# Bias tables read from one reversed line, memory projections ahead of the compressed branch, in a fused two-layer transformer step

## The chip, the cores and the metric

The kernel runs on one core of one Trainium2 chip. The metric is the device time of one execution in microseconds (us), lower is better; the kernel before takes 2472.95 us, the median of three runs.

## The reference, cut to what is computed

Two layers act on one sequence x of 512 positions by 1024 features, with a memory of 256 rows by 1024. The change touches the first layer, between its first feed-forward and its attention:

```python
def hybrid_layer(x, mem, ...):
    x = x + 0.5 * swiglu_ffn(rmsnorm(x, ffn1_norm_g), ffn1_w_in, ffn1_w_out)
    h = rmsnorm(x, mix_norm_g)
    q, kv, nsa_g, conv_in, q_mem, merge_g = jnp.split(h @ w_in, split_points, axis=-1)
    ...
    k_cmp = rmsnorm(compress(kc, cmp_pe_k, cmp_w1_k, cmp_w2_k), k_norm_g)
    v_cmp = compress(vc, cmp_pe_v, cmp_w1_v, cmp_w2_v)
    o_nsa = nsa_attention(q, k_cmp, v_cmp, ..., gates, rel_bias)
    o_conv = short_gated_conv(conv_in, conv_w, conv_b)
    o_mem = memory_attention(q_mem, mem, mem_norm_g, w_mem_kv, mem_q_norm_g, mem_k_norm_g)
    x = x + (g_nsa * o_nsa + g_conv * o_conv + g_mem * o_mem) @ w_out
    return x + 0.5 * swiglu_ffn(rmsnorm(x, ffn2_norm_g), ffn2_w_in, ffn2_w_out)

def memory_attention(q_mem, mem, mem_norm_g, w_mem_kv, q_g, k_g):
    km, vm = jnp.split(rmsnorm(mem, mem_norm_g) @ w_mem_kv, 2, axis=-1)
    km = rmsnorm(km.reshape(b, m, MEM_HEADS, MEM_HEAD_DIM), k_g)      # 4 heads of 256
    qm = rmsnorm(q_mem.reshape(b, s, MEM_HEADS, MEM_HEAD_DIM), q_g)
    sm = jnp.einsum('bshd,bmhd->bhsm', qm, km) * MEM_HEAD_DIM ** -0.5
    return jnp.einsum('bhsm,bmhd->bshd', jax.nn.softmax(sm), vm)
```

The scores of `nsa_attention` get a bias `rel_bias[rel_bucket(t - pos)]`, one value for each head and distance. The second layer has its own mixer and feed-forward (f3, after a cross attention); nothing of it is moved.

## The kernel before, in words

Activations lie transposed: eight tiles `X[k]` of 128 features by 512 positions. Each fp32 operand of a product is split into a high and a low part in a short float type (`split`, `w`), and a product is three matmuls: high by high, high by low, low by high. A weight unit of 128x1024 elements (512 KB) is loaded by SyncE's (SP's) DMA queue into one of three buffers `wr` (`raw`, L305), cast to `wh` by ScalarE (`copy`, L260), and `wl = wr - wh` is computed by GpSimd for two units of three and by VectorE for the third, inside the mixer (`wes`). `chunk` then issues 24 matmuls for one unit: of 512 columns for products with x, of 256 for products with the memory.

A scheduler puts the instructions of each engine in an order from the order of the program, the tile buffers and the priorities given; it may let an instruction come earlier than its place in the code. `tick` takes one closure from a list `todo` and runs it at the place of the call.

The stages that matter, in the order of time:

- `ffn("f1", ...)`: the first feed-forward, in three groups of hidden units. The last group's eight output products end at 362.5 us. `form_x` makes combinations of x for a Strassen-like product, early in a feed-forward.
- `mix1`, compressed branch (`compressed`): `cmp_src` makes four projections of x and multiplies each with the row factors `rb` of the norm; `cmp_blocks` writes VectorE's `zr` tiles from them; `compress` multiplies those with `cw1`. Between them `mem_q` makes the memory queries (`m1_qm`). Meanwhile `mem_prep` scales and splits the memory rows (`mh`, `ml`) and computes their norm, a step at each `tick` of `mem_q`.
- memory projections (`mem_kv`): eight units `m1_km` for the keys, eight `m1_vm` for the values, the sums of squares `ksq` for the keys' norm, and eight small products with `bm` that spread the norm's factors over the keys. At the ticks of the key units the bias tables are made (`tables`): a product of a one-hot array `oh1` with the bias table `rel` gives `drel`, a line of 640 values by head in DRAM; GpSimd's queue then copies the line to 128 rows of `dline` for each head, two heads to a DMA of 640 KB, eight DMAs. A second one-hot `oh2` gives `dcmp` for the compressed branch.
- memory heads (`mem_heads`): for each of four heads two gate units `m1_gm`, the scores (`softmax_mem`: VectorE's minimum, ScalarE's exponential `pm`), the transposes (`turn_mem`) and the product with the values. Query products of the attention follow, to 654.4 us.
- attention (`nsa`): 660 to 1120 us. `nsa_scores` loads for each head a tile `tab` of 128x512 biases, row p shifted by p, from `dline`, one head ahead (two buffers), and VectorE reads it once for each of the eight score tiles of a head (`sp<-s,tab`, L1274), adding it and taking the minimum in one pass.

## Time and profile before

| | |
|---|---|
| median of 3 runs | 2472.95 us (2469.25 to 2478.96) |
| the profiled execution | 2475.88 us, its span 2474.1 us |
| mean granted clock of TensorE | 0.977 of full speed |
| TensorE (PE) busy | 2373.4 us, 96% of the span |
| VectorE (DVE) busy | 1691.0 us, 68% |
| ScalarE (ACT) busy | 1160.3 us, 47% |
| GpSimd (POOL) busy | 435.1 us, 18% |

A row of a busy-time table gives, for a stretch, the busy time of each engine, the granted clock as a share of 2.4 GHz, the share of the DMA engines' time and what they moved. A row of a timeline is one instruction or a run of equal ones; in brackets stands the idle time of its engine before it and the instruction that ended that idle time. The durations of matmuls overlap, so their sum over a stretch is more than its length; how fast TensorE goes is read from how many lie in a stretch.

### The profile page before, as it was taken

Reading aid. Unit: us, or ns where it says so; the run is one execution under the profiler, and the core shown is the slowest. Engines: PE = TensorE matmul, PEld = TensorE weight load, DVE = VectorE, ACT = ScalarE, POOL = GpSimd, SP = SyncE. Lnnn points to the kernel's source line nnn. Section 1 sums busy time; section 2 is a strip of 40 time slices with the busy share of each in tenths; the row PEclk is TensorE's granted clock in tenths of the full one; section 3 lists DMA queues with packets and bytes.
Section 4 is the critical chain, followed back from the end, with each engine's and each line's share of the span. In section 5 each row is a group of like instructions: output and inputs, shape, how many; then the busy total and the mean of one; then the engine's idle time right before and its main releaser. Section 6 shows DMA issues by size and latency. Waiting matters only on the chain.

```text
span 2474.1 us, 35466 instructions
## 1 busy us (share of the span) xinstructions
PE 2373.4 (96%) x13618; PEld 2055.2 (83%) x13618; DVE 1691.0 (68%) x3150; ACT 1160.3 (47%) x2084; POOL 435.1 (18%) x266
## 2 busy tenths in 40 slices
PE   8999998969999999999999999998999998999997
PEld 6999987857777878787899898797788887899997
DVE  7766878544578676877767685467877357867675
ACT  6534453334355444554544353454655345644353
POOL 0000003331222223222000002121211431000000
PEclk9999999789999999999999999899999998999998
DMA  6545543352222222224455543122122332555551
GB/s 190 174 132 154 156 142 103 115 160 70 77 75 69 69 74 73 67 66 150 118 155 152 156 139 119 62 75 71 60 77 71 115 122 77 137 163 145 158 142 55
DMA packets 99486, 277.44 MB, mean 112 GB/s; under 512 B 18017, under 2 KB 26145, under 8 KB 99188
## 3 DMA queue, kind: packets, MB, share of 16 engines
q1 hardware_dynamic: 82660, 239.81, 29.6%
q0 software_dynamic: 16656, 35.36, 7.7%
q8 instruction: 107, 1.75, 0.3%
q14 instruction: 63, 0.52, 0.1%
HBM read 268.68 MB, written 11.64 MB: 113 GB/s over the span
## 4 chain that ended last, share of the span: by engine, by line
PE 64%; DVE 11%; ACT 3%; issue 3%; DMA 1%; POOL 1%; DVEq 0%; ACTq 0%; POOLq 0%
PE g L231 36%; PE s L231 12%; PE t L231 11%; PE o L231 3%; PE t L239 2%; DVE wl L242 2%; ACT wh L260 1%; DVE qk L242 1%; DMA wr<-f_s 0%; POOL wl L242 0%; DVE sp L1274 0%; DVE cv L254 0%; DMA wr<-m_gm 0%; DMA wr<-f_o 0%; DMA wr<-m_vm 0%
## 5 line engine op out<-in xcount | busy, mean ns | idle before, releaser
L231 PE MATMUL g<-xs,wh 128*128 128x512 f32 (+1 forms) x3022 | 875.9, 372 | 10.3 <-ACT wh L260 6.0
L260 ACT CAST wh<-wr 128x1024 fp32r<-128x1024 f32 (+6 forms) x405 | 409.9, 1016 | 612.8 <-PE g L231 217.9
L231 PEld LDWEIGHTS g<-xs,wh 128*128 128x128 f32 x3022 | 541.9, 190 | 100.7 <-ACT wh L260 11.2
L231 PE MATMUL g<-xs,wl 128*128 128x512 f32 (+1 forms) x1511 | 559.5, 370 | 1.9 <-POOL wl L242 1.2
L242 POOL TENSOR_TENSOR wl<-wr,wh 128x1024 fp32r<-128x1024 f32 (+4 forms) x135 | 313.0, 2320 | 918.0 <-ACT wh L260 754.9
L242 DVE TENSOR_TENSOR wl<-wr,wh 128x1024 fp32r<-128x1024 f32 (+5 forms) x270 | 327.1, 1213 | 65.8 <-ACT wh L260 63.4
L231 PEld LDWEIGHTS g<-xs,wl 128*128 128x128 f32 x1511 | 286.0, 189 | 51.1 <-issue 2.4
L231 PE MATMUL s<-xs,wh 128*128 128x256 f32 (+1 forms) x890 | 223.8, 340 | 5.5 <-ACT xs L260 2.0
L231 PE MATMUL t<-xs,wh 128*128 128x512 f32 (+1 forms) x888 | 222.2, 340 | 0.0
L565 POOL DMA_DIRECT2D wr<-f_s x57 | 49.4, 866 | 843.6 <-DMA wr<-f_s 232.1
L231 PEld LDWEIGHTS s<-xs,wh 128*128 128x128 f32 x890 | 153.2, 190 | 27.4 <-ACT wh L260 2.9
L231 PEld LDWEIGHTS t<-xs,wh 128*128 128x128 f32 x888 | 152.7, 189 | 18.6 <-ACT e L260 0.4
L231 PE MATMUL t<-xs,wl 128*128 128x512 f32 (+1 forms) x444 | 150.8, 340 | 2.7 <-DVE wl L242 2.7
L231 PE MATMUL s<-xs,wl 128*128 128x256 f32 (+1 forms) x445 | 150.4, 338 | 0.0
L257 ACT ACTIVATE sp<-sp,nm 128x128 f32<-128x128 f32 x192 | 101.9, 532 | 54.4 <-DVE nm L1274 41.6
L242 DVE TENSOR_TENSOR ptl<-t,pth 128x512 fp32r<-128x512 f32 (+1 forms) x128 | 73.4, 604 | 55.3 <-ACT pth L260 55.0
L260 ACT CAST pth<-t 128x512 fp32r<-128x512 f32 (+1 forms) x128 | 62.0, 520 | 92.4 <-PE t L239 92.0
L231 PEld LDWEIGHTS t<-xs,wl 128*128 128x128 f32 x444 | 83.7, 189 | 12.9 <-DVE wl L242 3.6
L231 PEld LDWEIGHTS s<-xs,wl 128*128 128x128 f32 x445 | 84.4, 190 | 8.9
L231 PE MATMUL g<-th,wl 128*128 128x256 f32 x308 | 86.6, 281 | 1.3 <-DVE wl L242 1.0
L231 PE MATMUL g<-th,wh 128*128 128x256 f32 x308 | 85.9, 279 | 1.3 <-DVE z L242 1.3
L231 PE MATMUL g<-tl,wh 128*128 128x256 f32 x308 | 85.7, 278 | 0.0
(525 smaller groups left out, 4834.1 us busy)
## 6 DMA issues: line engine op xcount, KB each, us to landing
wr<-f_ab SPq DMA_DIRECT2D x73, 512.0 KB, 3.7
wr<-f_s SPq DMA_DIRECT2D x57, 512.0 KB, 3.7
wr<-f_s POOLq DMA_DIRECT2D x57, 512.0 KB, 6.8
wr<-f_o SPq DMA_DIRECT2D x48, 448.0 KB, 3.5
wr<-m_f SPq DMA_DIRECT2D x40, 512.0 KB, 3.5
wr<-m_o SPq DMA_DIRECT2D x40, 512.0 KB, 3.5
w<-f_ab SPq DMA_DIRECT2D x57, 256.0 KB, 3.5
wr<-f_o SPq DMA_DIRECT2D x24, 512.0 KB, 4.1
```

Source lines behind the costliest of these rows:

```text
L231: self.pm = self.nc.tensor.matmul(o, l, r, start=first, stop=last, skip_group_check=more)
L239: self.nc.tensor.transpose(o, i, self.ident)
L242: (e or self.nc.vector).tensor_tensor(o, x, y, op=op)
L257: return self.nc.scalar.activation(o, x, f, **k)
L260: return self.nc.scalar.copy(o, x)
L565: nc.gpsimd.dma_start(rs, a[key + "_s"][c][:, D:], accum_op=ALU.add)
```

## The change

Five edits:

1. `oh1` is built reversed, so that the line of each head in `drel` runs the other way. `tab` is loaded straight from `drel`, row p starting at p, and the score pass reads it with a step of minus one. `dline` and its eight DMAs are gone. The four halves of the one-hots are loaded on SP's queue at the start of `tables`, and each half is multiplied, copied to a `row` and written to `drel` or `dcmp` by one small DMA of GpSimd's queue.
2. `ffn` gets a function `late` that it calls at the start of its last group of output products. `memory` opens there the pools of the memory and puts the steps of `mem_prep` and `tables` in `todo`, one for each output product's tick.
3. `mix1` runs `mem_kv` first, then `compressed`, then `mem_heads`. The row factors `rb` of x's norm are made behind the key units.
4. `cmp_src` makes two projections at a call, each scaled at once, in the `g` bank of PSUM, instead of four in rotating banks.
5. `form_x` hands out the forms of x two for each of the first units instead of all four behind the third; `mem_kv` and `mem_q` tick no more.

```diff
...
-    c["oh1"] = _onehot(511 - np.arange(LINE))
+    c["oh1"] = _onehot(np.arange(LINE) - 127)
...
     def tables(self, p):
 
         nc, a = self.nc, self.a
-        box = {}
-
-        def line(key, width, n):
+        rel = self.t(p, [33, 16], F32, "rel", 1)
+        nc.vector.memset(rel, 1.0)
+        nc.gpsimd.dma_start(rel[0:32], a["rel"])
+
+        def line(key, c, n, dst):
+            oh = self.t(p, [33, n], F32, "oh", 2)
+            nc.sync.dma_start(oh, a["c_" + key][:, c:c + n])
+
             def go():
-                if "rel" not in box:
-                    box["rel"] = self.t(p, [33, 16], F32, "rel", 1)
-                    nc.vector.memset(box["rel"], 1.0)
-                    nc.gpsimd.dma_start(box["rel"][0:32], a["rel"])
-                oh = self.load(key, pool=p)
-                box[key] = self.t(p, [16, 2 * width], F32, key + "l", 1)
-                for j in range(2):
-                    ps = self.ps("t", (16, width))
-                    s = slice(width * j, width * (j + 1))
-                    self.mm(ps, box["rel"], oh[:, s], True, True)
-                    nc.vector.tensor_copy(box[key][:, s], ps)
+                row = self.t(p, [16, n], F32, "row", 1)
+                ps = self.ps("t", (16, n))
+                self.mm(ps, rel, oh, True, True)
+                nc.vector.tensor_copy(row, ps)
+                nc.gpsimd.dma_start(dst[:, c:c + n], row)
             return go
 
-        def rows(j):
-            def go():
-                s = slice(2 * j, 2 * j + 2)
-                nc.gpsimd.dma_start(self.dline[s], self.drel[s, None, :].to_broadcast([2, P, LINE]))
-            return go
-
-        def cmpline():
-            nc.gpsimd.dma_start(self.drel, box["oh1"])
-            nc.gpsimd.dma_start(self.dcmp, box["oh2"])
-
-        st = [line("oh1", LINE // 2, 2), line("oh2", 512, 2), cmpline]
-        st += [rows(j) for j in range(8)]
+        st = []
+        for key, n, dst in (("oh1", LINE // 2, self.drel), ("oh2", 512, self.dcmp)):
+            st += [lambda c=c, a=(key, n, dst): line(a[0], c, *a[1:])() for c in (0, n)]
         return st
 
     def tick(self, n=1):
...
-    def ffn(self, key, scale, hook, np_):
+    def ffn(self, key, scale, hook, np_, late=lambda: None):
 
 
         fpool = self.pool("forms", "right")
...
                 last = gi == len(FGROUPS) - 1
                 if last:
                     fpool.__exit__(None, None, None)
+                    late()
                 if last and hook is None:
                     self.tail(p, f"{key}_o{gi}", uh, ul)
                     return
...
             wait, lag = [], 2
             for c in range(np_):
                 wait.append(self.plain(p, key, c, *parts[0], lag))
+                while len(self.B) < 2 * c:
+                    self.form_x(len(self.B))
                 if c >= lag:
                     while wait:
                         wait.pop(0)()
-                    while len(self.B) < 4 and (c == np_ - 1):
-                        self.form_x(len(self.B))
             n = FGROUPS[-1][1]
             prev = None
             for c in range(np_, n + 1):
...
                 self.chunk(ps, "m1_km", c, mh, ml)
                 k = self.t(q, [P, NMEM], F32, "kr", KT)
                 self.mul(k, ps, mrb)
-                self.tick()
                 kr.append(k)
                 s2 = self.t(q, [P, NMEM], F32, "ksq", 5)
                 self.act(s2, k, AF.Square)
...
                     sq.append(s2)
                 else:
                     self.tt(sq[-1], sq[-1], s2, ALU.add)
+            with self.tc.issue_after(self.pm.ins):
+                self.rb
             vh = [self.t(p, [P, D], F32R, f"vmh{i}", 1) for i in range(2)]
             vl = [self.t(p, [P, D], F32R, f"vml{i}", 1) for i in range(2)]
             for hf in range(2):
...
             qr.append(t)
             s2 = self.t(self.mp, [P, S], F32, "qsq", 5)
             self.act(s2, t, AF.Square)
-            self.tick()
             if c % 2 == 0:
                 self.qsq.append(s2)
             else:
...
         return out
 
 
-    def cmp_src(self, p):
-        ps = []
-        for c in range(4):
-            ps.append(self.psf())
-            self.chunk(ps[-1], "m1_c", c, self.xh, self.xl)
-            if c == 1:
-                self.behind(lambda: self.rc)
-            if c == 2:
-                self.behind(lambda: self.rb)
+    def cmp_src(self, p, kv):
         src = []
-        for c in range(4):
+        for c in range(2):
+            ps = self.ps("g")
+            self.chunk(ps, "m1_c", 2 * kv + c, self.xh, self.xl)
             t = self.t(p, [P, S], F32, "kcr", 4)
-            self.mul(t, ps[c], self.rb)
+            self.mul(t, ps, self.rb)
             src.append(t.rearrange("p (i l) -> p l i", l=16))
-        return src[:2], src[2:]
+        return src
 
     def cmp_blocks(self, p, kv, src):
 
...
         r, hl = h % 4, h % 8
         if br == 0:
             self.tab = self.t(p, [P, S], F32, "tab", 2)
-            dl = self.dline
-            nc.sync.dma_start(self.tab, bass.AP(tensor=dl.tensor, offset=dl.offset + h * P * LINE + 127,
-                                                ap=[[LINE - 1, P], [1, S]]))
+
+            dl = self.drel
+            nc.sync.dma_start(self.tab, bass.AP(tensor=dl.tensor, offset=dl.offset + h * LINE, ap=[[1, P], [1, S]]))
         kh, kl = kst[br]
         sp = self.t(p, [P, 1280], F32, "sp", 2)
         nm = self.t(p, [P, 4], F32, "nm", 4)
...
             self.mm(ps[:, :n], q, kh[:, :n], True, False)
             self.mm(ps[:, :n], q, kl[:, :n], False, True)
             x = sp[:, OFF[i]:OFF[i] + n]
-            nc.vector.tensor_tensor_reduce(x, ps[:, :n], self.tab[:, S - n:], op0=ALU.add, op1=ALU.min, scale=1.0,
+            nc.vector.tensor_tensor_reduce(x, ps[:, :n], self.tab[:, :n][:, ::-1], op0=ALU.add, op1=ALU.min, scale=1.0,
                                            scalar=3e38, accum_out=nm[:, i:i + 1])
             self.act(x, x, AF.Exp, scale=-1.0, bias=nm[:, i:i + 1], accum_out=sm[:, i:i + 1])
             if i == 1:
...
             self.nc.sync.dma_start(self.pe, self.a["pe"])
             self.vmask = self.load("vmask", pool=q)
             self.one128 = self.load("one128", pool=q)
-            sk, sv = self.cmp_src(q)
+            sk, sv = self.cmp_src(q, 0), self.cmp_src(q, 1)
             zk = self.cmp_blocks(q, 0, sk)
             qr = self.mem_q(0, 1)
 
...
-            with self.pool("memp") as mp, ExitStack() as es:
+            with self.pool("memp") as mp:
                 self.mp, self.qsq = mp, []
                 self.bm = self.const_r(mp, "bm")
-                keep = es.enter_context(self.pool("memkeep", "right"))
-                self.mem = {}
-                with self.pool("memtmp", "right") as tmp:
-                    self.todo = self.mem_prep(tmp, keep, "mem1", "memn", self.mem, True)
-                    qr = self.compressed()
-                    self.tick(len(self.todo))
-                with self.pool("memkv") as kv:
-                    with self.pool("tab", "right") as tab:
-                        self.todo = self.tables(tab)
-                        mem = self.mem_kv(kv)
-                        self.tick(len(self.todo))
-                    es.close()
-                    self.mem_heads(*qr, *mem)
+                mem = self.mem_kv(mp)
+                self.memkeep.close()
+                qr = self.compressed()
+                self.mem_heads(*qr, *mem)
...
-            self.dline = dp.tile([16, P, LINE], F32, name="dline")
             self.drel = dp.tile([16, LINE], F32, name="drel")
...
-            self.ffn("f1", 0.5, self.deferred(step, "mix", True), 3)
+            self.mem = {}
+
+            def memory():
+                self.memkeep, self.memtmp = ExitStack(), ExitStack()
+                keep = self.memkeep.enter_context(self.pool("memkeep", "right"))
+                tmp = self.memtmp.enter_context(self.pool("memtmp", "right"))
+                prep = self.mem_prep(tmp, keep, "mem1", "memn", self.mem, True)
+                tabs = self.tables(tmp)
+                self.todo = prep[:9] + tabs[:1] + prep[9:] + tabs[1:]
+
+            self.ffn("f1", 0.5, self.deferred(step, "mix", True), 3, memory)
+            self.memtmp.close()
             self.upool.__exit__(None, None, None)
```

How the order of instructions moves, at three places. The first is TensorE's order where f1's last output product (`t<-xs`) ends. `xs` is x in its two parts, `mh` and `ml` the memory's, `oh` a one-hot half. Before:

```order
L231 MATMUL t_3782<-xs_3505,wh_3784 128x512
L231 MATMUL t_3782<-xs_3506,wh_3784 128x512
L231 MATMUL t_3782<-xs_3505,wl_3785 128x512
L231 MATMUL g_3873<-xs_3543,wh_3875 128x512
L231 MATMUL g_3873<-xs_3544,wh_3875 128x512
L231 MATMUL g_3873<-xs_3543,wl_3876 128x512
L231 MATMUL g_3873<-xs_3580,wh_3875 128x512
L231 MATMUL g_3873<-xs_3581,wh_3875 128x512
L231 MATMUL g_3873<-xs_3580,wl_3876 128x512
```

With the change:

```order
L231 MATMUL t_3840<-xs_3504,wh_3842 128x512
L231 MATMUL t_3840<-xs_3505,wh_3842 128x512
L231 MATMUL t_3840<-xs_3504,wl_3843 128x512
L231 MATMUL o_3886<-ones_113,macc_3515 128x2 x2
L231 MATMUL t_3911<-oh_3908,rel_3518 16x320
L231 MATMUL g_3981<-mh_3553,wh_3983 128x256
L231 MATMUL g_3981<-ml_3554,wh_3983 128x256
L231 MATMUL g_3981<-mh_3553,wl_3984 128x256
L231 MATMUL t_3925<-oh_3922,rel_3518 16x320
L231 MATMUL g_3981<-mh_3598,wh_3983 128x256
L231 MATMUL g_3981<-ml_3599,wh_3983 128x256
L231 MATMUL g_3981<-mh_3598,wl_3984 128x256
```

The first product behind f1 was the compressed branch's with x; it is now the first key unit of the memory, with the table products between its first matmuls.

The second is GpSimd's order; `wl` is the subtraction for a weight unit, and the rows of "DMA" are transfers that this engine issues. Before, beside the memory projections:

```order
L538 DMA drel<-oh1l_4807 16x640
L242 TENSOR_TENSOR wl_4938<-wr_4936,wh_4937 128x1024
L534 DMA dline<-drel 256x1x640
L539 DMA dcmp<-oh2l_4851 16x1024
L534 DMA dline<-drel 256x1x640
L242 TENSOR_TENSOR wl_4974<-wr_4972,wh_4973 128x1024
L534 DMA dline<-drel 256x1x640 x2
L242 TENSOR_TENSOR wl_5047<-wr_5045,wh_5046 128x1024
L534 DMA dline<-drel 256x1x640
L242 TENSOR_TENSOR wl_5089<-wr_5087,wh_5088 128x1024
```

With the change, at the end of f1 and the start of the memory projections:

```order
L516 DMA rel_3518<-rel 32x16
L242 TENSOR_TENSOR wl_3984<-wr_3982,wh_3983 128x1024
L242 TENSOR_TENSOR wl_4055<-wr_4053,wh_4054 128x1024
L527 DMA drel<-row_3910 16x320
L527 DMA drel<-row_3924 16x320
L242 TENSOR_TENSOR wl_4090<-wr_4088,wh_4089 128x1024
L527 DMA dcmp<-row_3931 16x512
L527 DMA dcmp<-row_3938 16x512
L242 TENSOR_TENSOR wl_4161<-wr_4159,wh_4160 128x1024
L242 TENSOR_TENSOR wl_4197<-wr_4195,wh_4196 128x1024
```

The row copies `dline` are gone from between the subtractions; four small transfers stand between the first subtractions instead, and from there on only subtractions follow.

The third is TensorE's order in the memory heads; `s` are scores of a head, `g` with `xs` the gate units, `t<-ident` transposes and `o` the products with the values. Before:

```order
L231 MATMUL s_5443<-kml_5284,qh_5413 128x256
L231 MATMUL s_5443<-kmh_5283,ql_5414 128x256
L231 MATMUL s_5443<-kmh_5290,qh_5417 128x256
L231 MATMUL s_5443<-kml_5291,qh_5417 128x256
L231 MATMUL s_5443<-kmh_5290,ql_5418 128x256
L231 MATMUL s_5583<-kmh_5297,qh_5572 128x256
L231 MATMUL s_5583<-kml_5298,qh_5572 128x256
L231 MATMUL s_5583<-kmh_5297,ql_5573 128x256
L231 MATMUL s_5583<-kmh_5304,qh_5576 128x256
```

With the change:

```order
L231 MATMUL s_5435<-kmh_4509,ql_5410 128x256
L231 MATMUL g_5496<-xs_3559,wh_5498 128x512
L231 MATMUL g_5496<-xs_3560,wh_5498 128x512
L231 MATMUL g_5496<-xs_3559,wl_5499 128x512
L231 MATMUL g_5496<-xs_3603,wh_5498 128x512
L231 MATMUL g_5496<-xs_3604,wh_5498 128x512
L231 MATMUL g_5496<-xs_3603,wl_5499 128x512
L231 MATMUL g_5496<-xs_3649,wh_5498 128x512
L231 MATMUL g_5496<-xs_3650,wh_5498 128x512
L231 MATMUL g_5496<-xs_3649,wl_5499 128x512
L231 MATMUL g_5496<-xs_3695,wh_5498 128x512
L231 MATMUL s_5416<-kmh_4502,qh_5405 128x256
```

Before, the scores of two heads stood one behind the other with no gate unit between them; now ten matmuls of a gate unit lie between the two sets of scores of one head.

## Rows read from the trace of the kernel before

**Rows 1.** Busy time by stretch (first line: its columns)

```profile
core 0: us, PE busy (x) PEld busy (x) DVE busy (x) ACT busy (x) POOL busy (x), PEclk, DMA share, GB/s
362.50:457.70 95.20, 85.42 (x425) 70.83 (x424) 72.01 (x125) 32.59 (x44) 29.11 (x15) 0.98 0.35 115
457.70:541.20 83.50, 68.22 (x332) 56.97 (x332) 33.05 (x77) 22.29 (x39) 28.70 (x18) 0.69 0.42 131
541.20:638.80 97.60, 88.69 (x425) 71.31 (x424) 45.83 (x94) 39.48 (x74) 23.56 (x11) 0.98 0.27 83
660.00:1120.00 460.00, 445.08 (x2325) 366.72 (x2324) 342.01 (x811) 227.59 (x504) 126.13 (x66) 1.00 0.23 71
```

**Rows 2.** PE by form, three stretches: xcount, busy us, mean ns, idle before

```profile
L231 PE MATMUL g<-xs,wh 128*128 128x512 f32 x160 | 51.6, 402 | 6.4 <-DVE x L242 2.7 <-ACT wh L260 2.3 <-DVE xs L254 0.7
L231 PE MATMUL g<-ml,wh 128*128 128x256 f32 x64 | 22.1, 347 | 0.0
L231 PE MATMUL t<-im,qsq 128*128 128x4 f32 x26 | 3.4, 267 | 0.0
L231 PE MATMUL g<-xs,wh 128*128 128x512 f32 x136 | 43.3, 397 | 3.3 <-ACT wh L260 3.3
```

**Rows 3.** Chain that ended last, whole span: start us, us, what

```profile
1167.27 5.44 PE g L231 x24
```

**Rows 4.** Busy time by stretch, 4 us each, in the memory projections

```profile
484.00:488.00 4.00, 4.00 (x21) 4.00 (x20) 0.00 (x0) 0.00 (x0) 1.59 (x2) 0.50 0.79 175
488.00:492.00 4.00, 4.00 (x35) 4.00 (x35) 0.85 (x2) 2.16 (x3) 2.52 (x2) 1.00 0.29 103
```

**Rows 5.** Timeline of POOL from 500 us: start, us, instruction, idle before

```profile
501.59 1.05 POOL L534 DMA_DIRECT2D dline<-drel  x1 [8.67 <-PE g L231]
502.66 2.35 POOL L242 TENSOR_TENSOR wl<-wr,wh 128x1024 fp32r<-128x1024 f32 x1
```

**Rows 6.** Timeline of PE from 500 us, same columns

```profile
505.07 0.58 PE L231 MATMUL g<-mh,wl 128*128 128x256 f32 x1 [2.80 <-POOL wl L242]
...
516.80 2.30 PE L231 MATMUL t<-im,ksq 128*128 128x4 f32 x10 [7.33 <-DVE ksq L242]
```

**Rows 7.** DMA issues, 440 to 560 us: xcount, KB, us to landing

```profile
dline<-drel POOLq DMA_DIRECT2D x8, 640.0 KB, 18.4
wr<-m_km SPq DMA_DIRECT2D x8, 512.0 KB, 3.9
wr<-m_vm SPq DMA_DIRECT2D x8, 512.0 KB, 6.5
```

**Rows 8.** By tile tab: landing of the loads of the bias tables

```profile
DMA to landing us min/median/max: 2.6/3.2/3.8
```

**Rows 9.** By tile: ns min/median/max; last by line, 360 to 440 us

```profile
L1274 DVE CUSTOM_DVE_ANT_0 sp<-s,tab x128: 275/484/695, 672.9 to 1113.6; 128x128 f32<-128x128 f32 x32, 128x256 f32<-128x256 f32 x32, 128x384 f32<-128x384 f32 x32, 128x512 f32<-128x512 f32 x32
...
L242 DVE TENSOR_TENSOR ws<-sq,sq x12: 416/418/419, 24.2 to 2138.2; 128x256 f32<-128x256 f32 x12
...
L242 DVE TENSOR_TENSOR zr<-kcr,pe 64x256 f32<-64x256 f32 x16 | 15.7, 984 | 0.2
```

**Rows 10.** By tile mraw: first and last start of the memory's scaling

```profile
L257 ACT ACTIVATE mh<-mraw,cols x16: 491/495/507, 334.7 to 2040.5; 128x256 fp32r<-128x256 f32 x16
```

**Rows 11.** Timeline of PE from 40 us

```profile
51.18 0.58 PE L231 MATMUL s<-th,wh 128*128 128x256 f32 x1 [4.52 <-DVE z L242]
```

**Rows 12.** Chain that ended last from 540 to 585 us

```profile
555.19 1.05 ACT wh L260
...
560.72 0.66 ACT pm L257 x2
...
565.55 1.05 DVE pm L249 x4
```

**Rows 13.** Timeline of PE from 400 us

```profile
413.75 0.73 PE L231 MATMUL g<-xs,wh 128*128 128x512 f32 x2 [2.33 <-ACT wh L260]
```

**Rows 14.** Who PE waited for, 300 to 660 us: total, times, longest

```profile
PE s L231 <- ACT pm L257: 5.0, 7, 1.4
```

## The prediction

> **What bounds the kernel now.** I read the busy time of the engines by stretch first, to find where TensorE is not at work or not at speed; then TensorE's instructions by form, to count the work of a stretch; then the timelines and waits, for what held it up; last the changed order of instructions.
>
> TensorE bounds the kernel, and the attention shows what a good stretch looks like: of 460.00 us it is busy 445.08, at clock 1.00, while VectorE is busy 342.01 [rows 1]. The three stretches ahead of it are the ones whose order changes, and they are worse: TensorE's busy times 85.42, 68.22 and 88.69 leave 9.8 + 15.3 + 8.9 = 34.0 us idle. In the memory projections the clock is 0.69 besides. With two levels, 1.2 and 2.4 GHz, a mean of 0.69 means that a share s = (1 - 0.69)/0.5 = 0.62 of the stretch was at the lower; applied to 68.22 us of busy time, 42 us ran at half speed, and half of that, 21 us, is lost.
>
> What the work needs at full clock: 24 matmuls of 512 columns take 5.44 us, 0.227 each [rows 3]. Of 256 columns, 35 fit in 4 us at clock 1.00, 0.114 each, and 21 at 0.50 [rows 4]. Counting the forms, of which one or two stand for each stretch in [rows 2]:
> - compressed branch: 289 of 512 columns (160, 80, 16, 16, 9, 8), 65.6 us; 96 of 256, 10.9; some 40 short ones, 3 (estimate). Sum 79.5 of 95.2, so **15.7 lost**.
> - memory projections: 192 of 256 columns (three forms of 64), 21.9; 52 of 512, 11.8; some 85 short ones, 8. Sum 41.7 of 83.5, **41.8 lost**: 15.3 idle, 21 clock, 5 in gaps too short to be listed.
> - memory heads: 297 of 512 columns (136, 67, 48, 46), 67.4; 96 of 256, 10.9; 32 transposes, 2.3. Sum 80.6 of 97.6, **17.0 lost**.
> Together 74.5 us. The matmuls are the same in number after the change, so it can only win back from this, or lose elsewhere.
>
> **The change, part by part.**
>
> *The tables.* Before, GpSimd stands at a `dline` DMA for 8.67 us with a weight subtraction of 2.35 us behind it [rows 5]; TensorE then waits 2.80 us for that `wl` [rows 6]. The eight DMAs carry 8 x 640 = 5120 KB and land in 18.4 us; beside them value weights land in 6.5 us, against 3.9 for key weights [rows 7]. Removed: eight issues of 1.05 us on GpSimd, 8.4 us, and the traffic. Added: four small DMAs at the same issue price, 4.2 us, ahead of the third subtraction, and four loads on SP's queue ahead of f1's last products. These fall while that group still runs on weights already loaded, so at most one SP issue delays a load; a load of this size lands in 2.6 to 3.8 us [rows 8] and f1's product of at least 5.44 us covers it. I price the added part at nothing; without that cover it is four times 3.2, 13 us at most.
>
> *The reversed read.* In the attention VectorE reads `tab` 128 times, 484 ns median, 62 us in all [rows 9]. No row shows a read with a step of minus one over consecutive words. The lower end is 0: the same number of elements with the same two operands. The upper end is the reversed and widely strided read of `zr`, 984 ns mean for 64x256, against 418 for a plain 128x256 addition: 2.35 times, which on 62 us is 84 us. I take 0, because the new read touches neighbouring words, and in that is nearer to the plain row; the 84 stays for the slower rival. The Trainium skill, "SBUF — State Buffer", section "Door 1: The DMA port swizzle", says that accesses within a 16-byte line run at full rate and each new line costs; by that the step of one word is free and the sum stays, while `zr`'s stride pays on every element, as its row has it. The "Vector Engine (DVE) Microarchitecture Reference", section "5.1 Performance modes — why throughput varies by op and dtype", in the same Trainium skill lists the streaming of a negative step as not measured; no run here shows it.
>
> *The memory's norm beside f1.* `mh` already starts at 334.7 us, ahead of f1's end at 362.5 [rows 1, 10]: the scheduler had brought it forward. Worth 0.
>
> *The forms of x.* A few VectorE and ScalarE instructions swap early in f1, where TensorE waits 4.52 us for VectorE's `z` [rows 11]. The `z` itself stays where it is. Worth 0, within 2 us either way.
>
> *The order of the mixer.* This carries the sum.
> - Memory projections. In the old order they came behind the short products of the compressed branch (26 of 4 columns alone [rows 2]), and the clock was half at 484 and full at 488 [rows 4]. Now they come right behind f1's matmuls of 512 columns, so I expect full clock. The keys' norm is a chain: TensorE waits 7.33 us for `ksq` [rows 6], then for `mr2y` and for the rows spread by `bm`. In the changed order 18 matmuls of the next branch, 4.1 us, stand between the norm's products and its transposes, and more between the `bm` products. What stays lost: the row factors and x's cast at the start, 2; the weight feed, 4; the rest of the chain, 3.5. So 9.5 of 41.8 stays, **-32**.
> - Weight feed, the check on those 4 us: a unit occupies one of three buffers for landing 3.9, cast 1.05 and subtraction 2.35 [rows 5, 7, 12], 7.3 us, 2.4 per unit, below the 24 x 0.114 = 2.7 that TensorE needs. With the landing of 6.5 it would be 9.9/3 = 3.3, above it.
> - Compressed branch. TensorE waited 6.4 us there on x's normalised tiles and weights [rows 2]. The first of it, right behind f1, is now covered by the memory projections; the wait for a cast, 2.33 us at 413.75 [rows 13], and those on `zr`'s VectorE run stay. Half of 15.7 goes: **-8**.
> - Memory heads. Waits on `pm`, 5.0 us in seven, longest 1.4 [rows 14], come from scores of two heads back to back; the chain holds four exponentials, 0.66 us for two, and four scalings, 1.05 in all [rows 12]: 2.4 us. Ten gate matmuls, 2.3 us, now lie between the two sets of scores, against those 2.4. 6 of 17.0 stays: **-11**.
>
> Sum -32 - 8 - 11 = **-51**. From 2475.88 us of the profiled execution that is 2425; from the median of the runs, 2.9 lower, 2422. I forecast **2424 us**.
>
> **The rivals.**
> - *The half clock stays in the memory projections.* Had the weights to be waited for at each unit (3.3 against 2.7 us), TensorE would work in short bursts, and the 21 us of the clock would not come back: 2424 + 21 = 2445. For it: the values' landing of 6.5 and that GpSimd still does two of three subtractions; against it: the 5 MB of row copies that slowed the landing are gone. [...]
> - *The heads' chain stays open.* Cover 2.3 against chain 2.4 is close; if nothing comes back there, 2424 + 11 = 2435. With the first rival too, 2456.
> - *The losses only move.* The compressed branch now follows the projections and has its own weights and VectorE runs; if its start waits as long as the projections did, the time stays at about 2473. Against it: x's tiles have some 60 us more to be ready.
> - *Slower: the reversed read.* If VectorE reads backwards at `zr`'s rate, 84 us are added in the attention, where each score tile waits for that pass and its exponential. VectorE has 460 - 342 = 118 us of slack there, but not at those places; all exposed it gives 2424 + 84 = 2508. It becomes slower than before once over 61 us are exposed, that is from a factor of 2.0 on (62 us more).
>
> **How the numbers follow.** A measurement here can tell 0.5% from no change, 12 us: bounds 2460.6 and 2485.3. Chances: the forecast 0.60; half clock 0.17 (2445, with the heads 2456); heads alone 0.09; losses that move 0.05; the reversed read 0.04; better than the range 0.05. The range goes from 2404, where 71 of the 74.5 us are won, to 2456, both of the first rivals; it leaves out 0.14. Faster 0.60 + 0.17 + 0.09 + 0.05 = 0.91, same 0.05, slower 0.04.
>
> **What would show it.** Right: clock above 0.9 from 362 to 425 us; no GpSimd idle time over 5 us before a DMA there; the projections' stretch near 51 us, the value weights' landing near 4; attention still 460 us with `sp<-s,tab` at 484 ns. Wrong: a clock of 0.5 in the key units, waits of TensorE on `wl` or `wh` at each unit, waits on `pm` still 5 us, or `sp` near 1 us. The forecast fails as a whole if the three stretches, up to 638.8 us before, end later than about 620.

## The result, and the profile after

The changed kernel takes 2456.31 us (median; 2450.72 to 2457.26) against 2474.0 for the kernel before (2469.25 to 2478.96; a fourth run has joined the three): a ratio of 0.9924, 95% interval 0.9899 to 0.9949, about 18 us less. The forecast was 2424, 51 less; 2456.31 also lies just above the range. The direction was right, the size was not.

The profiled execution spans 2455.5 us. First the busy time by stretch (columns as in [rows 1]): key and value projections with the first products of the compressed branch, the rest of that branch, the memory heads.

```profile
362.50:431.00 68.50, 62.72 (x368) 52.86 (x367) 46.26 (x82) 25.78 (x38) 30.91 (x16) 0.95 0.45 146
431.00:541.00 110.00, 101.10 (x475) 82.19 (x475) 84.06 (x130) 39.12 (x59) 36.85 (x15) 0.92 0.31 99
541.00:612.00 71.00, 66.77 (x337) 53.51 (x336) 40.46 (x82) 29.60 (x61) 12.49 (x6) 0.98 0.21 61
```

The clock of the projections went from 0.69 to 0.95. VectorE, though, is busy 84.06 of 110 us in the second stretch. The waits of TensorE there and ahead of it, in its timeline (answering to [rows 6, 11, 13]):

```profile
50.53 0.58 PE L231 MATMUL s<-th,wh 128*128 128x256 f32 x1 [4.28 <-DVE z L242]
...
368.27 1.25 PE L231 MATMUL t<-oh,rel 33*16 33x320 f32 x2 [3.09 <-DVE u L242]
...
461.80 0.79 PE L231 MATMUL g<-xs,wl 128*128 128x512 f32 x1 [2.69 <-DVE wl L242]
...
487.48 0.73 PE L231 MATMUL g<-xs,wh 128*128 128x512 f32 x2 [2.21 <-ACT wh L260]
489.92 0.79 PE L231 MATMUL g<-xs,wl 128*128 128x512 f32 x1 [1.71 <-POOL wl L242]
```

The wait of 7.33 us for `ksq` is gone; waits on the compressed branch's weights have come. By tile, the read of the tables and the memory's scaling ([rows 9, 10]):

```profile
L1259 DVE CUSTOM_DVE_ANT_0 sp<-s,tab x128: 275/484/693, 647.7 to 1091.2; 128x128 f32<-128x128 f32 x32, 128x256 f32<-128x256 f32 x32, 128x384 f32<-128x384 f32 x32, 128x512 f32<-128x512 f32 x32
...
L257 ACT ACTIVATE mh<-mraw,cols x16: 493/495/503, 336.3 to 2018.2; 128x256 fp32r<-128x256 f32 x16
```

Read backwards, a table costs 484 ns at the median, as it did forwards. The value weights land in 3.4 us ([rows 7] had 6.5):

```profile
wr<-m_vm SPq DMA_DIRECT2D x8, 512.0 KB, 3.4
```

To compare kernels I add up one figure from the windows of 4 us, from 362.5 us (f1's last product, where all agree within about 1 us) to the first score that reads a table: TensorE's idle time, and its busy time times one minus the clock.

| kernel | stretch, us | idle | lost to the clock | rest |
|---|---|---|---|---|
| before | 310.4 | 36.2 | 22.7 | 251.5 |
| changed | 285.2 | 21.1 | 12.0 | 252.1 |
| tables alone (e1) | 275.1 | 15.4 | 8.0 | 251.7 |
| order alone (e2) | 303.7 | 31.9 | 21.3 | 250.5 |
| tables alone, copies put back (e7) | 310.4 | 43.7 | 14.1 | 252.6 |
| tables alone, memory part on VectorE (b3) | 264.6 | 8.3 | 4.8 | 251.5 |

The rest is 250.5 to 252.6 us in all of them: the work itself. So before the change 59 us could be won, not 74.5. Each row is one profiled execution; that of e7 is the fastest of its ten runs (2470.96 us, 13 below their median).

### The profile page after: what moved, and what is told of

The parts are those of the page before. It is cut to its first block, busy times and chain, and to the rows that moved or that the text cites. A ratio compares the mean times of both kernels' runs of the same rounds, so it can differ in the third digit from the quotient of the medians.

```text
span 2455.5 us, 35462 instructions
## 1 busy us (share of the span) xinstructions
PE 2365.4 (96%) x13618; PEld 2048.3 (83%) x13618; DVE 1710.2 (70%) x3150; ACT 1160.2 (47%) x2084; POOL 431.6 (18%) x260
## 4 chain that ended last, share of the span: by engine, by line
PE 63%; DVE 11%; ACT 2%; issue 2%; DMA 1%; POOL 0%; DVEq 0%; ACTq 0%; POOLq 0%
PE g L231 36%; PE s L231 12%; PE t L231 10%; PE o L231 3%; PE t L239 2%; DVE wl L242 2%; ACT wh L260 1%; DVE qk L242 1%; DMA wr<-f_s 1%; DVE sp L1259 0%; DMA wr<-f_o 0%; DVE cv L254 0%; DVE o L254 0%; POOL wl L242 0%; DVE xs L242 0%
## 5 line engine op out<-in xcount | busy, mean ns | idle before, releaser
L231 PE MATMUL g<-xs,wh 128*128 128x512 f32 (+1 forms) x3064 | 900.6, 376 | 7.4 <-ACT wh L260 3.0
L231 PEld LDWEIGHTS g<-xs,wh 128*128 128x128 f32 x3064 | 555.1, 192 | 100.1 <-ACT wh L260 3.5
L231 PE MATMUL g<-xs,wl 128*128 128x512 f32 (+1 forms) x1532 | 573.2, 374 | 6.3 <-POOL wl L242 3.6
L242 DVE TENSOR_TENSOR wl<-wr,wh 128x1024 fp32r<-128x1024 f32 (+6 forms) x270 | 326.5, 1211 | 69.9 <-ACT wh L260 67.4
L231 PEld LDWEIGHTS g<-xs,wl 128*128 128x128 f32 x1532 | 293.2, 191 | 58.6 <-POOL wl L242 4.9
L231 PE MATMUL t<-xs,wh 128*128 128x512 f32 (+1 forms) x860 | 213.2, 337 | 0.1
L231 PE MATMUL t<-xs,wl 128*128 128x512 f32 (+1 forms) x430 | 145.4, 338 | 3.7 <-DVE wl L242 3.7
```

Source lines behind the costliest of these rows:

```text
L231: self.pm = self.nc.tensor.matmul(o, l, r, start=first, stop=last, skip_group_check=more)
L242: (e or self.nc.vector).tensor_tensor(o, x, y, op=op)
```

## The experiments

All times below are medians against the kernel before on the same chip, with the ratio's 95% interval.

**The tables alone (e1).** Edit 1 in the old kernel, the new `tables` called where the old one was, at the key units' ticks; nothing else:

```diff
-    c["oh1"] = _onehot(511 - np.arange(LINE))
+    c["oh1"] = _onehot(np.arange(LINE) - 127)
...
-            self.dline = dp.tile([16, P, LINE], F32, name="dline")
...
```

> The kernel before with the reversed line alone (no rows in DRAM, tab read backwards), its old order of stages kept. Theory A (the order of the mixer carries the gain, the tables a few us): 2468 to 2472 us against 2474, the memory projections' clock still near 0.7, the wait for ksq still above 5 us. Rival B (the row copies on GpSimd's queue made the weights late, and so the waits and the low clock): 2455 to 2460 us, the projections' clock above 0.9. Either way sp<-s,tab stays at 484 ns.

Measured 2446.7 us, ratio 0.9882 (0.9865 to 0.9899): 31 us less, more than the whole change gives and more than the 2455 to 2460 of rival B. **My theory A fell.** The memory projections, still behind the compressed branch's short products, now run at clock 0.98:

```profile
461.70:537.00 75.30, 75.11 (x433) 62.77 (x433) 41.25 (x85) 31.48 (x50) 35.04 (x18) 0.98 0.47 144
```

Not all of this can be laid to the copies. In the kernel before, the longest stretch at half clock starts near 460 us, right behind 26 products of four columns for the norm of the memory queries, with TensorE busy throughout; the first row copy is issued only at 482.89 us. A line of TensorE, one of GpSimd, then the busy time of 458 to 488 us before and in e1:

```profile
458.26 3.41 PE L231 MATMUL t<-im,qsq 128*128 128x4 f32 x26
482.89 1.11 POOL L534 DMA_DIRECT2D dline<-drel  x1
458.00:488.00 30.00, 30.00 (x131) 24.29 (x130) 14.20 (x35) 6.80 (x13) 10.23 (x7) 0.55 0.35 97
458.00:488.00 30.00, 30.00 (x214) 26.56 (x214) 16.09 (x38) 12.78 (x21) 11.32 (x7) 0.94 0.45 139
```

The clock falls within or right behind these 26 products in every profile taken here; what differs is how long it stays down: 27 us before (13.6 lost), some 3 us in e1 and in e7 below (1.7 lost). It differs between executions of one and the same kernel, too. Kernel b1 (below, no copies) was profiled twice, at 2439.25 and at 2428.57 us:

```profile
452.00:472.00 20.00, 20.00 (x103) 18.89 (x103) 10.89 (x29) 5.38 (x11) 5.32 (x3) 0.57 0.33 93
452.00:472.00 20.00, 20.00 (x143) 17.78 (x143) 13.77 (x35) 8.72 (x15) 8.28 (x5) 0.91 0.40 118
```

So 12 of the 30 us between the profiled executions of before and e1 (spans 2474.1 and 2444.5) lie in a stretch of half clock that began ahead of the copies. An estimate from the spans less that loss: the copies cost 18 us before and 25 in e7, against 31 and 37 by the medians. What sets the length of that stretch stays open.

**The order alone (e2).** The changed kernel with the old tables at the key units' ticks:

```diff
...
-                mem = self.mem_kv(mp)
+                with self.pool("tab", "right") as tab:
+                    self.todo = self.tables(tab)
+                    mem = self.mem_kv(mp)
+                    self.tick(len(self.todo))
...
```

> The changed kernel with the old tables put back: the line not reversed, eight row copies at the ticks of the key units, tab read forwards; the new order of stages kept. Theory A: 2458 to 2464 us, the clock of the projections above 0.9. Rival B: 2468 us or more, the value weights landing in 6 us or more, TensorE waiting for wl or wh at the value units.

2476.39 us, 0.9991 (0.9977 to 1.0005): no difference. The low clock and the wait for `ksq` are there in the new order too: the stretch in which the changed kernel has clock 0.95, and TensorE's wait in it.

```profile
362.50:431.00 68.50, 52.46 (x281) 41.84 (x280) 35.24 (x87) 20.22 (x35) 22.14 (x15) 0.78 0.49 144
410.27 2.29 PE L231 MATMUL t<-im,ksq 128*128 128x4 f32 x10 [6.55 <-DVE ksq L242]
```

**The forms of x (e3)**, handed out as before:

```diff
-                while len(self.B) < 2 * c:
-                    self.form_x(len(self.B))
...
+                    while len(self.B) < 4 and (c == np_ - 1):
+                        self.form_x(len(self.B))
```

> The changed kernel with the forms of x handed out as before, all four behind the third unit. If that edit is worth nothing: 2456 us within 4, the wait for z at 51 us 4.5 against 4.3 us. If the slower first 350 us of the changed kernel's profile (1 us more, clock 0.95 against 0.98 in the first 100) come from it: 2452 us or less.

2457.32 us, 0.9918 (0.9902 to 0.9935), the changed kernel's time: worth nothing.

**The tables' bank (e4).**

```diff
-                ps = self.ps("t", (16, n))
+                ps = self.ps("o", (16, n))
```

> The changed kernel with the tables' products in PSUM's bank o instead of t. In the changed kernel TensorE waits 3.09 us for VectorE's u before the first of them, since f1's last product lies in bank t. If that wait is the bank's: it goes, and the half clock behind it (368 to 372 us) with it, 2451 us. If VectorE's queue itself is late there (row copies, norm of x), the wait moves to the next key unit: 2456 us.

2456.59 us, 0.9913 (0.9891 to 0.9935). The wait of 3.09 us for `u` is gone, but 1.8 us for `rsv` at the same place and 0.8 for `row` a little later are new (a wait of 1.8 us for `rsl` near 405 us is in both): VectorE's queue itself is late there.

**The copies put back (e7)**, into e1; nothing reads them:

```diff
+        st += [rows(j) for j in range(8)]
```

> The tables-alone kernel (2446.7 us) with the eight row copies to DRAM put back behind the four line steps, though nothing reads them. Theory C (the copies themselves: GpSimd's queue held up, weights landing late, then waits and the low clock): 2465 us or more, value weights landing in 6 us or more. Theory D (what cost the time was the old way of making the line: one-hots loaded late, four table products in a bunch): 2447 to 2452 us.

2483.94 us, 1.0021 (1.0004 to 1.0038): the 31 us are lost again, and 6 more. Part of how stands in three timelines of this kernel, GpSimd, VectorE and TensorE:

```profile
500.13 0.50 POOL L527 DMA_DIRECT2D dcmp<-row  x1 [14.28 <-DVE row L526]
500.95 1.12 POOL L533 DMA_DIRECT2D dline<-drel  x1 [0.32 <-issue]
502.09 2.36 POOL L242 TENSOR_TENSOR wl<-wr,wh 128x1024 fp32r<-128x1024 f32 x1
```

```profile
485.37 1.21 DVE L242 TENSOR_TENSOR wl<-wr,wh 128x1024 fp32r<-128x1024 f32 x1
499.16 0.68 DVE L526 COPY row<-t 16x512 f32<-16x512 f32 x1 [12.58 <-DMA dcmp<-row]
499.76 0.40 DVE L242 TENSOR_TENSOR kr<-g,rmb 128x256 f32<-128x256 f32 x1
```

```profile
500.31 0.76 PE L231 MATMUL g<-wh,mh 128*128 128x512 f32 x1 [8.97 <-DVE kr L242]
504.50 0.58 PE L231 MATMUL g<-mh,wl 128*128 128x256 f32 x1 [1.72 <-POOL wl L242]
515.67 2.29 PE L231 MATMUL t<-im,ksq 128*128 128x4 f32 x10 [6.16 <-DVE ksq L242]
```

The first transfer of `dcmp` lands late behind the copies (18.5 us each). VectorE waits 12.58 us to reuse its `row`, with the scaling of keys (`kr`) queued behind; TensorE waits 8.97 us for that. GpSimd stands too, with a subtraction behind it. Before the change only the second arm existed, since the lines were not reused. That arm is longer than [rows 5, 6] let it seem. The chain that ended last in the kernel before, from 492 us on (its longer pieces), runs from GpSimd's stand through a weight's load to the wait for `ksq`:

```profile
492.92 8.65 issue
501.61 1.03 POOL dline L534
502.66 2.37 POOL wl L242
505.04 7.86 DMA wr<-m_vm
513.95 0.42 ACT ksq L257
514.39 2.36 DVE ksq L242
516.80 2.31 PE t L231 x10
```

`issue` is time in which the profile shows nothing that GpSimd waited for. The late subtraction frees its buffer `wr` late; a value weight loads into it and lands 7.86 us later (the median in e1 is 3.6); ScalarE stands 8.45 us for it, and the square `ksq` is queued behind that cast. So in the kernel before a slow landing is a link of the chain that GpSimd's queue began.

**The copies, with no weight behind them (e14).** e7 with the subtractions of projections and heads on VectorE:

```diff
+                self.wes = [nc.vector]
                 with self.pool("memkv") as kv:
...
                     self.mem_heads(*qr, *mem)
+                self.wes = [nc.gpsimd, nc.gpsimd, nc.vector]
```

> The tables alone with the row copies put back (2484 us), and in the memory projections and heads every weight subtraction on VectorE, so that no weight stands behind a copy in GpSimd's queue. Theory G (GpSimd stands at the copies, and the subtractions and row buffers behind them are what TensorE waits for): 2455 us or less. Theory H (the copies' traffic makes the weights land late): 2465 us or more, value weights still landing in 6 us or more, TensorE's waits on wh.

2449.45 us, 0.9897 (0.9874 to 0.9919): theory G. GpSimd now stands 59 us at a transfer and no engine waits for it; the value weights land as late as ever; yet TensorE is busy 82.41 of 83.5 us:

```profile
546.01 0.50 POOL L527 DMA_DIRECT2D dcmp<-row  x1 [59.14 <-DVE row L526]
```

```profile
wr<-m_vm SPq DMA_DIRECT2D x8, 512.0 KB, 7.4
```

```profile
457.70:541.20 83.50, 82.41 (x467) 68.79 (x466) 52.59 (x100) 33.26 (x50) 3.69 (x5) 0.96 0.53 159
```

So a slow landing alone costs TensorE next to nothing here; the copies' cost needs the queue they are issued from. Two things limit this. The edit also let the scheduler put the last line's product later, so VectorE's arm and GpSimd's arm are not told apart by it, and only two of the eight copies are issued before 546 us, the others behind the projections. And VectorE's subtraction of 1.22 us instead of 2.4 frees the weight buffers sooner, which may itself help against a slow landing.

**The old stage order (e9).** The changed kernel with `compressed` ahead of `mem_kv` again. With it go the four projections of `cmp_src` and the old place of `rb`, so that "the order" here and in b5 is edits 3 and 4 together:

```diff
...
-                mem = self.mem_kv(mp)
-                self.memkeep.close()
                 qr = self.compressed()
-                self.mem_heads(*qr, *mem)
+                with self.pool("memkv") as kv:
+                    mem = self.mem_kv(kv)
+                    self.memkeep.close()
+                    self.mem_heads(*qr, *mem)
```

> The changed kernel with compressed branch and memory projections in the order of before (and the four projections of cmp_src as before); tables and memory norm stay beside f1's last product, forms of x as changed. If the new order of the stages costs the 10 us by which the changed kernel is slower than the tables alone: 2446 us within 4. If the place of tables and memory norm beside f1 costs them: 2456 us within 4.

2452.86 us, 0.9894 (0.9875 to 0.9913). The median falls to the second expectation, but by its interval it can't be told from the changed kernel or from e1. It settles nothing; b5, below, repeats the question without GpSimd's disturbance and answers it the other way.

**Who subtracts in the compressed branch (e5, e6).** The edit of e5; e6 has `[nc.gpsimd]` in its first line.

```diff
+                self.wes = [nc.vector]
                 qr = self.compressed()
+                self.wes = [nc.gpsimd, nc.gpsimd, nc.vector]
```

> The changed kernel with all weight subtractions of the compressed branch on VectorE (1.22 us each) instead of two of three on GpSimd (2.4 us). Theory E (VectorE is late there because its instructions wait while GpSimd subtracts, zr and zl taking up to 3 us): 2450 us or less, zr's longest below 1 us. Theory F (VectorE simply has too much work there): 2460 us or more.

> The changed kernel with all weight subtractions of the compressed branch on GpSimd. Theory F: 2450 us or less, since VectorE loses some five subtractions of 1.22 us. Theory E: 2458 us or more, more of VectorE's instructions at 2 to 3 us.

On VectorE 2445.84 us, 0.9871 (0.9857 to 0.9886); on GpSimd 2457.82, 0.9914 (0.9894 to 0.9935), the changed kernel's time. Giving VectorE more work makes the kernel faster, and from 362.5 us to the attention VectorE itself is busy for less time, 181.18 us in 340 instructions against 189.25 in 327: theory E. One rival is not separated: on VectorE a subtraction takes 1.22 us and not 2.4, so each weight is also ready sooner. By tile (ns, min/median/max), the changed kernel, then e5:

```profile
L242 DVE TENSOR_TENSOR zr<-kcr,pe x32: 560/606/2604, 445.1 to 485.5; 64x256 f32<-64x256 f32 x16, 64x248 f32<-64x248 f32 x16
...
L242 DVE TENSOR_TENSOR zl<-zr,zh x4: 1222/1900/3056, 453.8 to 490.7; 128x1024 fp32r<-128x1024 f32 x4
```

```profile
L242 DVE TENSOR_TENSOR zr<-kcr,pe x32: 584/605/623, 443.7 to 478.9; 64x256 f32<-64x256 f32 x16, 64x248 f32<-64x248 f32 x16
...
L242 DVE TENSOR_TENSOR zl<-zr,zh x4: 1217/1220/1222, 450.5 to 484.1; 128x1024 fp32r<-128x1024 f32 x4
```

And in the changed kernel's timelines the long ones lie under a subtraction on GpSimd:

```profile
478.59 2.54 DVE L242 TENSOR_TENSOR zr<-kcr,pe 64x248 f32<-64x248 f32 x1
...
490.66 3.06 DVE L242 TENSOR_TENSOR zl<-zr,zh 128x1024 fp32r<-128x1024 f32 x1
```

```profile
477.92 2.82 POOL L242 TENSOR_TENSOR wl<-wr,wh 128x1024 fp32r<-128x1024 f32 x1 [0.51 <-ACT wh L260]
...
487.50 5.14 POOL L242 TENSOR_TENSOR wl<-wr,wh 128x1024 fp32r<-128x1024 f32 x2 [6.76 <-ACT wh L260]
```

The `zr` from 478.59 ends at 481.13, the subtraction from 477.92 at 480.74. The Trainium skill, "SBUF — State Buffer", section "Who interferes with whom", states that a VectorE instruction with two SBUF inputs and a GpSimd instruction that reads SBUF block each other, whichever comes second waiting until the other ends; the trace agrees (2604 ns at the longest beside GpSimd, 623 without).

**The same in the old order (b1, b3).** b1 is e1 with e5's edit; b3 keeps the subtractions on VectorE to the end of the memory heads. **b2** is e5 with the tables made at the key units' ticks.

> The tables alone (2446.7 us) with the compressed branch's weight subtractions on VectorE. If GpSimd's subtractions slow VectorE there as in the changed kernel (zr's longest 2.6 us in both): 2440 us or less. If the old order has cover enough for it: 2447 us within 4.

> The tables alone with the weight subtractions on VectorE from the compressed branch to the end of the memory heads. If VectorE has room for them (41 of 75 us busy in the projections): 2438 us or less; if it is late with the keys and values then: 2445 us or more.

> The changed kernel with the compressed branch's weight subtractions on VectorE (2445.8 us) and the tables made at the ticks of the key units instead of beside f1's last product. If the tables beside f1 hold up VectorE and TensorE there (3.1 us of wait, 2.6 of half clock in the changed kernel): 2441 us or less. If not: 2446 us within 4.

b1: 2435.36 us, 0.9833 (0.9815 to 0.985): 11 us less than e1, so the old order had no cover for GpSimd's subtractions either. b3: 2433.0 us, 0.9825 (0.981 to 0.984), the fastest here though not told apart from b1, 44 us ahead of the kernel before and beyond the changed one; its projections, in the window of before:

```profile
457.70:541.20 83.50, 83.47 (x464) 69.41 (x463) 58.25 (x115) 40.44 (x65) 1.95 (x4) 0.98 0.44 130
```

b2: 2451.81 us, 0.9901 (0.9883 to 0.9919), 6 us slower than e5 and outside both expectations. A wait of 4.9 us for `rsh` shows now; that the table products had been filling it is likely, but not shown.

**Order or place (b5, with e5 and b1 again beside it).** b5 is e9 with e5's edit.

> The changed kernel with the stages in their old order, tables and memory norm still beside f1's last product, and the compressed branch's weight subtractions on VectorE. Beside it stand the tables alone with the same subtractions (2435.4 us: old order, nothing beside f1) and the changed kernel with them (2445.8 us: new order, both beside f1). If the place beside f1 costs most of these 10 us: 2442 us or more. If the order of the stages does: 2438 us or less.

> The changed kernel with the compressed branch's weight subtractions on VectorE once more, on the same chip as the old order, so that the two can be compared: 2446 us within 3.

> The tables alone with the same subtractions, on the same chip: 2435 us within 3.

b5 2437.91 us, 0.9819 (0.9795 to 0.9842); e5 2447.04, 0.9856 (0.9833 to 0.9879); b1 2435.63, 0.982 (0.9796 to 0.9844). The place beside f1 costs 2 us, which can't be told from nothing; the new order of the stages costs 2447.04 - 2437.91 = 9 us. Of that, 7.5 lie ahead of the attention (274.8 against 267.3): 2.4 idle, 1.5 clock, 3.6 in what the table calls the rest. This split is not firm: the first profile of e5, as long (274.5), has 9.8 us of clock loss where this one has 6.2. The waits that only the new order has are for the row factors and f1's last results (`rsl` 2.4, `u` 2.0); those on `pm` are 3.9 against 1.7.

## Why the prediction was wrong, point by point

- *The loss that could be won*, 74.5 us: too large. The idle time and the clock were right (34.0 and 21); the other 19.5 us, of which I called 5 gaps too short to be listed, are not lost time. Every kernel in the table keeps 250.5 to 252.6 us of the stretch as work, b3 too, whose projections are almost without waits. Whether I had put the short matmuls too low or the cadence of the others too even, no run separates.
- *"The order of the mixer. This carries the sum."* This is the step that failed. The tables carry it: 31 us alone, where I gave their removal no term of its own. The order gives nothing with the old tables (e2) and costs 9 us with the new ones. In the sum -32 for the projections stood under the order. That size came out, by luck: the changed kernel's first stretch loses 5.8 us idle and 3 to the clock, 9 against the 9.5 that were to stay; e2, with the order and the old tables, still loses 16 and 12 there. The rows that said so were on the page: GpSimd standing 8.67 us at a copy, a subtraction behind it, TensorE waiting [rows 5, 6]. Of that stand I named only the one wait that ended on `wl`, 2.80 us, and not what came of it: the weight loaded late, the square behind it, hence `ksq` at 7.33 us, the exposed chain of the norm, and the clock that fell in that idle time.
- *The half clock*. I had laid it to the short products ahead of the projections. For its larger part that holds (13.6 of 22.7 us lost, from 460 us on); but the low stretch goes where these products go, to 526 us in the changed kernel (3.4 us lost), and how long it lasts is not set by the order, as e1 and the two profiles of b1 show. The rest of the loss before came with waits, most of it from 512 to 532 us, with and behind the wait for `ksq`.
- *Compressed branch, -8*: the sign was wrong. That stretch (431 to 541 us) now loses 8.9 us idle and 8 to the clock, 17 against 11.5 before by the same count and the 8 that were to stay. GpSimd's subtractions stretch `zr` there and moving them wins 10 us (e5), but they did so in the old order as well (2605 ns at the longest before; b1 wins 11 us), so they don't explain why the new order is slower. I had taken `zr`'s mean of 984 ns [rows 9] for the price of its stride; without GpSimd beside it that mean is 613 (e5).
- *Memory heads, -11*: right in size (4.2 us idle and 1.3 of clock in that stretch, against 6 that were to stay) and in its mechanism. In the changed kernel two heads have eight or ten gate matmuls between their sets of scores and next to no wait, two have only four, and there TensorE waits:

```profile
566.21 0.38 PE L231 MATMUL s<-kmh,qh 128*128 128x256 f32 x1 [1.75 <-ACT pm L257]
606.01 0.38 PE L231 MATMUL s<-kmh,qh 128*128 128x256 f32 x1 [1.75 <-ACT pm L257]
```

  But it isn't the order of the stages that brings the gate matmuls there: in e1, the old order, they stand between the scores too, with one wait of 1.7 us on `pm`.
- *Right*: the reversed read costs nothing (484 and 484 ns), so the slower rival was out; the memory's norm already lay beside f1 (336.3 against 334.7 us); the forms of x are worth nothing. The rival of late weights was half right: a slow landing was a link of the chain before, but e14 has weights landing in 7.4 us and next to no wait.
- Of the 32 us by which the profiled change (18.6 us) falls short of 51, 16 had never been lost, 10 more stay lost than forecast (33.1 against 74.5 - 51 = 23.5), and 7 lie from the first score on. These 7 are not shown to be the change's doing: behind the attention, profiles of all these kernels take 1354.8 to 1367.4 us, and b1 alone 1360.6 and 1356.1. My sign of failing, the three stretches ending later than about 620 us, was too wide: the first score came 25.2 us earlier, which puts that end near 614.
- Step by step from before to e1, to the place beside f1, to the new order, the parts are -31, +2 and +9: -20 against -18 measured. They don't simply add on another path: with the old tables, order and place together are worth 1 us (e2).

## What to carry to other kernels

Before pricing a transfer by its bytes, look at which engine issues it and what stands behind it in that engine's queue: here eight copies cost 31 us by the medians because weight subtractions, and in e7 a reused buffer, stood behind them, and little once no weight did (e14). When a change holds several edits, take the largest wait's whole chain of consequences to the edit that removes its first link, and do not share it out by stage. A work-sharing between VectorE and GpSimd is worth testing with all of it on VectorE: a subtraction of 2.4 us on the one can hold up the other as long. And where the clock's low stretches differ from one execution to the next, compare medians of several runs, and use a profile for what waits on what.

## What the runs showed of the hardware that was not expected

- Instructions of VectorE with two operands in SBUF (`zr`, `zl`) took 2.5 to 3.1 us where they met a GpSimd subtraction, and 0.6 to 1.2 without; giving VectorE GpSimd's share of the subtractions in the compressed branch made the kernel 10 us faster.
- A reversed read of consecutive words costs VectorE nothing (128 instructions, 484 ns median both ways).
- In all profiles here the granted clock falls to its lower level within or right behind 26 products of four columns, before with TensorE busy without a gap (30.00 of 30.00 us). It stays there for 27 us before and some 3 in e1, and for 17 and 3 us in two executions of the same kernel (b1).
